# A two-layer decoder trunk: decay tables in another layout, the skip diagonal on ScalarE, and other hands for the last norms

## The chip, the cores and the metric

The kernel runs on one core of a Trainium2 chip. The metric is the device time of one execution in microseconds; before the change the median of three runs is 2406.37 us. Within a core five engines run their own instruction rows and meet at semaphores: TensorE (PE, matrix products), VectorE (DVE), ScalarE (ACT), GpSimd (POOL) and SyncE (SP, which issues DMAs).

## The reference, cut to what matters

The input x is 1024 tokens by 1024 channels, float32. The first layer is a diagonal state-space layer (S5), the second is stick-breaking attention; behind each stand a norm, a squared-ReLU MLP (1024 to 4096 to 1024) and another norm.

```python
def layer_norm(x, g, b):
    mu = jnp.mean(xf, axis=-1, keepdims=True)
    var = jnp.mean(jnp.square(xf - mu), axis=-1, keepdims=True)
    return (xf - mu) * lax.rsqrt(var + LN_EPS) * g + b

def s5_mixer(x, ...):
    u = (x @ w_in).reshape(bsz, seq, S5_GROUPS, S5_GROUP)      # 64 groups of 16 channels
    ...                                                        # a = exp(lambda dt), B scaled
    _, _, s_re, s_im = lax.associative_scan(combine, (a_re, a_im, bu_re, bu_im), axis=0)
    y = einsum(s_re, c_re) - einsum(s_im, c_im) + d_skip * u
    g = jax.nn.gelu(y)
    return (g * jax.nn.sigmoid(g @ w_glu + b_glu)) @ w_out

for layer in range(2):
    mix = s5_mixer(...) if layer == 0 else stick_breaking_attention(...)
    x = layer_norm(alpha * x + mix, ln_mix_g, ln_mix_b)
    ff = square(relu(x @ w1 + b1)) @ w2 + b2
    x = layer_norm(alpha * x + ff, ln_mlp_g, ln_mlp_b)
```

## The kernel before

Every float32 product is made of three matmuls on operands split into a high and a low part; `split` (L122 the cast of the high part on ScalarE, L123 the subtraction for the low part on VectorE) is the most used helper. The stages follow each other: the projection u (to 58.6 us of the profiled span), the S5 loop (to about 262), the gate (GLU, to 365), the projection `so` with its norms (to 457), the MLP of layer 0 (`m0` up, `d0` down, to about 1040 and its norms), K, V and attention (to 1650), the projection `ao` with its norms (to 1740), and the MLP of layer 1 (`m1` up, `d1` down). A scheduler orders each engine's row from the order of the code and the readiness of the operands; an engine then runs its row strictly in order.

**S5 loop.** The 64 groups are worked through in 16 halves of four groups (`Half`), two for each of eight indices i. Rotation tables C and S for index i come from `outer_tables(i)` (L480 to L491): four products and two sums of [128, 4, 8, 16] on VectorE, whose factors TA (8 powers) and TB (16 powers) are broadcast along the other's axis. TA and TB are built once (L413 to L420) by doubling, with `cmul` (L364 to L369: four products, a difference and a sum on VectorE) on 1, 2, 4 (and for TB 8) powers at a time for all NQ = 32 columns. They stand as [P, power, NQ], so that neighbouring powers lie 128 bytes apart.

A half's chain is: VT and WW (L526 to L528, VectorE, from the input coefficients), their transposes pv (TensorE) and copies V, Vs (L542 to L544, ScalarE), p = V x U (L590, L592, TensorE), R (L596 to L598, VectorE), the scan (L603, VectorE), Rs and Rc (L610, L611, VectorE), y (L616 to L619, TensorE), its gelu and its transposed output. Beside it, `decay` and `kern` make the short kernel matrix: a diagonal `di` [32, 4, 32] of d_skip values (L555, VectorE) and products of VT and WW are summed in the PSUM tile pk (L563 to L568) and copied into Dm (L576, four ScalarE copies), which the y products read. While the first six indices of the loop run, TensorE is filled up with matmuls of the projection u.

**Up-projection.** `mlp_up` multiplies with Strassen-like sums: `xo.first`, `xo.second` and `xo.third` transpose blocks of y into operands B.. and T.. of the products, `early(q)` is one 12-matmul product (M1 into bank A for even q, M2 into a bank of `psX` for odd q) made ahead of the main loop, while the norms of the last tiles still run. `xo.third` uses `psX` banks too.

**Down-projection and last norms.** `run` in the down stage makes products M1, M5, M6, M3, M7, M2, M4, each added by VectorE (`evict`, L1105) to the half tiles of y0..y7. Each norm has `stats` (L182, one per half tile), `center` (L187 to L190 on VectorE, the power on GpSimd, L192, the mean's subtraction on ScalarE, L194) and `scale` (L203 times rs and g, L204 plus b, both VectorE, then the DMA out, L206). In layer 1, y0..y3 are complete after M3 and their norms run under M7 and M4, from `queue`; y4..y7 follow as M4 ends bank by bank.

## Time and profile before

| | |
|---|---|
| median of 3 runs | 2406.37 us (2405.84 to 2408.62) |
| the profiled execution | 2409.81 us |
| its span, first to last instruction | 2408.1 us |
| mean granted TensorE clock | 0.981 |
| TensorE busy | 2283.8 us, 95% |
| VectorE busy | 1853.5 us, 77% |
| ScalarE busy | 1220.4 us, 51% |
| GpSimd busy | 409.1 us, 17% |

Rows are read so: a timeline row has start, duration, engine, line, operation, the tile written, the tiles read, the shape and, in brackets, how long the engine had waited for whom. Instructions of one engine overlap a little in the records, so that a step's true price is the distance to the next start.

### The profile page before, as it was taken

The numbers are of one execution on the slowest core, as the hardware profiler recorded it, in microseconds if no ns is written. First come the engines' busy times: TensorE is split into PE (matmuls) and PEld (weight loads), VectorE is DVE, ScalarE is ACT, GpSimd is POOL, SyncE is SP. The second block draws the span as 40 slices with busy tenths as digits, with TensorE's granted clock in tenths as the row PEclk, the third lists the DMA queues.
The fourth block names the chain that finished last, engine by engine and source line by source line (L and its number), as shares of the span: only waits on it lengthen the run. The fifth ranks groups of instructions, "written<-read, shape, count | busy, mean of one in ns | idle before, by whom it ended". The sixth has DMA issues, their size and how long they took to land.

```text
span 2408.1 us, 32696 instructions
## 1 busy us (share of the span) xinstructions
PE 2283.8 (95%) x11072; PEld 1873.7 (78%) x11072; DVE 1853.5 (77%) x2899; ACT 1220.4 (51%) x2299; POOL 409.1 (17%) x704
## 2 busy tenths in 40 slices
PE   9987899999999999999999999888989999999996
PEld 7777787777888788888887888766777888788885
DVE  7899674886665787789169999896887666687888
ACT  5455441465555444445156777663356555444443
POOL 4000140012111000001144434341002111100001
PEclk9998999999999999999999999999999999999998
DMA  4221232376444845437655554555457343665432
GB/s 147 61 78 47 60 111 66 136 257 206 145 144 149 303 134 154 148 97 192 123 134 117 129 122 109 119 140 192 139 173 280 147 152 145 228 201 167 135 110 105
DMA packets 195160, 349.38 MB, mean 145 GB/s; under 512 B 23216, under 2 KB 66224, under 8 KB 194992
## 3 DMA queue, kind: packets, MB, share of 16 engines
q1 hardware_dynamic: 136112, 246.61, 32.4%
q0 software_dynamic: 58880, 100.69, 15.1%
q8 instruction: 87, 1.43, 0.3%
q14 instruction: 81, 0.66, 0.1%
HBM read 212.96 MB, written 100.66 MB: 130 GB/s over the span
## 4 chain that ended last, share of the span: by engine, by line
PE 65%; DVE 16%; issue 9%; DMA 4%; ACT 3%; POOL 2%; SPq 0%; POOLq 0%; DVEq 0%; ACTq 0%
PE d0M L1096 4%; PE d0M L1097 4%; PE d0M L1098 4%; PE d1M L1096 4%; PE d1M L1098 4%; PE d1M L1097 4%; DVE qq L1447 2%; PE m0A L832 2%; PE m0A L833 2%; PE m0A L834 2%; PE m1A L832 2%; PE m1A L834 2%; PE m1A L833 2%; DVE be L1448 2%; PE po L1474 2%
## 5 line engine op out<-in xcount | busy, mean ns | idle before, releaser
L1447 DVE TENSOR_TENSOR_SCAN qq<-qq 128x128 f32<-128x128 f32 (+7 forms) x128 | 173.7, 1359 | 12.1 <-POOL qq L1441 11.9
L1096 PE MATMUL d1M<-w_d12M,w_d1HM 128*128 128x512 f32 x448 | 175.7, 393 | 3.9 <-DVE d1y L1105 3.9
L1098 PE MATMUL d1M<-w_d12M,w_d1HM 128*128 128x512 f32 x448 | 175.9, 393 | 0.0
L1096 PE MATMUL d0M<-w_d02M,w_d0HM 128*128 128x512 f32 x448 | 174.7, 391 | 1.2 <-DVE d0y L1105 1.2
L1097 PE MATMUL d1M<-w_d12M,w_d1HM 128*128 128x512 f32 x448 | 175.4, 392 | 0.0
L1097 PE MATMUL d0M<-w_d02M,w_d0HM 128*128 128x512 f32 x448 | 174.8, 390 | 0.0
L1098 PE MATMUL d0M<-w_d02M,w_d0HM 128*128 128x512 f32 x448 | 174.6, 390 | 0.0
L122 ACT CAST w_d1HM<-d1hM 128x512 fp32r<-128x512 f32 x110 | 68.3, 621 | 170.1 <-PE d1M L1098 148.1
L122 ACT CAST w_d0HM<-d0hM 128x512 fp32r<-128x512 f32 x110 | 68.3, 621 | 169.0 <-PE d0M L1098 142.8
L122 ACT CAST wTh<-pt 128x512 fp32r<-128x512 f32 (+1 forms) x192 | 88.1, 486 | 84.1 <-PE pt L1460 83.6
L1460 PE MATMUL pt<-ident,be 128*128 128x128 f32 x576 | 91.2, 283 | 36.4 <-DVE wTl L123 28.0
L192 POOL TENSOR_TENSOR rsd<-ved,nhalf 128x1 f32<-128x1 f32 x16 | 16.2, 1014 | 621.1 <-DVE ved L190 612.9
L1460 PEld LDWEIGHTS pt<-ident,be 128*128 128x128 f32 x576 | 70.3, 144 | 62.1 <-issue 17.8
L123 DVE TENSOR_TENSOR w_d1HM<-d1hM,w_d1HM 128x512 fp32r<-128x512 f32 x110 | 75.8, 689 | 52.3 <-ACT w_d1HM L122 52.2
L123 DVE TENSOR_TENSOR w_d0HM<-d0hM,w_d0HM 128x512 fp32r<-128x512 f32 x110 | 75.9, 690 | 51.5 <-ACT w_d0HM L122 51.4
L123 DVE TENSOR_TENSOR wTl<-pt,wTh 128x512 fp32r<-128x512 f32 (+1 forms) x192 | 99.7, 545 | 11.5 <-ACT wTh L122 11.4
L1448 DVE TENSOR_TENSOR be<-be,qq 128x127 f32<-128x127 f32 (+7 forms) x128 | 99.4, 777 | 7.2 <-POOL be L1441 0.5
L1096 PEld LDWEIGHTS d1M<-w_d12M,w_d1HM 128*128 128x128 f32 x448 | 84.4, 188 | 24.1 <-ACT w_d12M L122 4.3
L1438 ACT ACTIVATE qq<-pz 128x512 f32<-128x512 f32 (+1 forms) x192 | 97.2, 507 | 10.9 <-DVE be L1448 5.3
L1096 PEld LDWEIGHTS d0M<-w_d02M,w_d0HM 128*128 128x128 f32 x448 | 84.1, 188 | 21.2 <-DVE d0y L1105 2.5
L1098 PEld LDWEIGHTS d1M<-w_d12M,w_d1HM 128*128 128x128 f32 x448 | 84.6, 189 | 18.4
L1097 PEld LDWEIGHTS d1M<-w_d12M,w_d1HM 128*128 128x128 f32 x448 | 84.6, 189 | 17.9
(480 smaller groups left out, 7084.5 us busy)
## 6 DMA issues: line engine op xcount, KB each, us to landing
d0hM<-h_d SPq DMA_DIRECT2D x110, 256.0 KB, 2.7
d1hM<-h_d SPq DMA_DIRECT2D x110, 256.0 KB, 2.7
x1ring<-in_w SPq DMA_DIRECT2D x70, 256.0 KB, 3.1
x3ring<-in_w SPq DMA_DIRECT2D x70, 256.0 KB, 3.2
h_d<-m0hs POOLq DMA_DIRECT2D x64, 256.0 KB, 2.8
h_d<-m1hs POOLq DMA_DIRECT2D x64, 256.0 KB, 2.8
d0r<-in_w SPq DMA_DIRECT2D x58, 256.0 KB, 3.7
d1r<-in_w SPq DMA_DIRECT2D x58, 256.0 KB, 3.3
```

The costliest lines, as they stand in the source:

```text
L122: act.copy(hi, src)
L123: dve.tensor_sub(lo, src, hi)
L832: pe.matmul(ps_, wh, xh[:, k], start=first and k == 0, stop=False, skip_group_check=True)
L833: pe.matmul(ps_, wh, xl[:, k], start=False, stop=False, skip_group_check=True)
L834: pe.matmul(ps_, wl, xh[:, k], start=False, stop=k == 3, skip_group_check=True)
L1096: pe.matmul(ps_, hh[:, tok(t)], wh, start=first, stop=False, skip_group_check=True)
L1097: pe.matmul(ps_, hh[:, tok(t)], wl, start=False, stop=False, skip_group_check=True)
L1098: pe.matmul(ps_, hl[:, tok(t)], wh, start=False, stop=last, skip_group_check=True)
L1438: act.activation(qq[:, s0:s1], pz, AF.Sigmoid, scale=-0.125)
L1447: dve.tensor_tensor_scan(out=rev, data0=rev, data1=rev, initial=1.0, op0=ALU.mult, op1=ALU.bypass)
L1448: dve.tensor_mul(be[:, 0:ns - 1], be[:, 0:ns - 1], qq[:, 1:ns])
L1460: pe.transpose(pt[:, b_], self.be[:, tok(s0 + b_)], ident)
```

## The change

1. TA and TB become [P, NQ, power]: the inner index of `outer_tables` is adjacent; `cmul` writes and reads them through a rearranged view.
2. `di` is written by four ScalarE activations of [32, 32] (the identity times a per-partition d_skip) instead of one VectorE product of [32, 128].
3. In `mlp_up`, `early(1)` stands before `xo.third(..., 4)` and `early(2)` before `xo.third(..., 5)`.
4. Last norms of both down stages: the statistics of the halves n = 0 of y0..y3 run when M5's products are issued (`bnst` gets 8 buffers), only the other half's after the last sum.
5. Last norms of layer 1 only: g is copied by ScalarE into two PSUM tiles, the scaling runs in halves with g from there; the bias of y0..y4 is added by GpSimd (one 128x1024 instruction), that of y5..y7 by VectorE in halves with a DMA for each. g and b are loaded at M2 rather than M3, and the entries of `queue` are spread over eight units.

```diff
 class LayerNorm:
-        def __init__(self, pl, y, g, b, nm, last=False, dst=None):
+        def __init__(self, pl, y, g, b, nm, last=False, dst=None, gp=None, late=False):
...
-            self.st = pl.tile([P, 2, 6], F32, tag="bnst", name=f"st{nm}", bufs=4)
+            self.gp, self.late = gp, late
+            self.st = pl.tile([P, 2, 6], F32, tag="bnst", name=f"st{nm}", bufs=8)
...
         def scale(self):
             y = self.y
-            for c in self.parts():
+            for h in range(2) if self.gp else ():
+                c = half(h)
+                dve.scalar_tensor_tensor(y[:, c], y[:, c], self.rs, self.gp[h], op0=ALU.mult, op1=ALU.mult)
+                if self.late:
+                    dve.tensor_add(y[:, c], y[:, c], self.b[:, c])
+                    dma.dma_start(self.dst[:, c], y[:, c])
+            if self.gp and not self.late:
+                pool.tensor_add(y, y, self.b)
+                dma.dma_start(self.dst, y)
+            for c in self.parts() if not self.gp else ():
                 dve.scalar_tensor_tensor(y[:, c], y[:, c], self.rs, self.g[:, c], op0=ALU.mult, op1=ALU.mult)
                 dve.tensor_add(y[:, c], y[:, c], self.b[:, c])
...
-        TA = [sp.tile([P, 8, NQ], F32, name=f"TA{x}") for x in range(2)]
-        TB = [sp.tile([P, 16, NQ], F32, name=f"TB{x}") for x in range(2)]
+        TA = [sp.tile([P, NQ, 8], F32, name=f"TA{x}") for x in range(2)]
+        TB = [sp.tile([P, NQ, 16], F32, name=f"TB{x}") for x in range(2)]
         for tab, n_, s0 in ((TB, 4, 1), (TA, 3, 5)):
+            tab = [v.rearrange("p q a -> p a q") for v in tab]
...
-            a_ = [v[:, :, qs].rearrange("p a q -> p q a").unsqueeze(3).to_broadcast(sh) for v in TA]
-            b_ = [v[:, :, qs].rearrange("p b q -> p q b").unsqueeze(2).to_broadcast(sh) for v in TB]
+            a_ = [v[:, qs].unsqueeze(3).to_broadcast(sh) for v in TA]
+            b_ = [v[:, qs].unsqueeze(2).to_broadcast(sh) for v in TB]
...
-                dve.tensor_mul(di[self.hh][0:32], ident[0:32, 0:32].unsqueeze(1).to_broadcast([32, 4, 32]),
-                               dsk[:, self.g0:self.g0 + 4].unsqueeze(2).to_broadcast([32, 4, 32]))
+                for q in range(4):
+                    act.activation(di[self.hh][0:32, q], ident[0:32, 0:32], AF.Copy,
+                                   scale=dsk[:, self.g0 + q:self.g0 + q + 1])
...
         early(0)
+        early(1)
         xo.third(psX, "p", y_tiles, 4)
         rest[0]()
         w_early(4, wb)
         w_early(5, wb)
-        early(1)
         rest[1]()
+        early(2)
         xo.third(psX, "p", y_tiles, 5)
-        early(2)
...
             def ln(t):
-                lns[t] = LayerNorm(cp, self.y[t], gb[0], gb[1], f"{nm}{t}", t == 7, (out if self.last else x2_d)[tok(t)])
+                lns[t] = LayerNorm(cp, self.y[t], gb[0], gb[1], f"{nm}{t}", t == 7,
+                                   (out if self.last else x2_d)[tok(t)], gp, t > 4)
             def ln_a(t):
-                if t not in lns:
-                    ln(t)
-                    lns[t].stats()
+                lns[t].stats(1)
                 lns[t].center()
...
-                if fin and m == "M3" and q == 0:
+                if fin and m == "M2" and q == 0:
                     gb = [bcast(cp, A[f"lnf{x}"][l], f"{nm}{x}") for x in "gb"]
...
-                        queue = [[(ln_a, 0)], [(ln_a, 1), (ls, 0)], [(ln_a, 2), (ls, 1)], [(ln_a, 3), (ls, 2)],
+                        gp = [psC.tile([P, HF], F32, tag="p", name=f"{nm}g{h}") for h in range(2)]
+                        for h in range(2):
+                            act.copy(gp[h], gb[0][:, half(h)])
+                        for t in range(4):
+                            lns[t].gp = gp
+                        queue = [[(ln_a, 0)], [(ls, 0)], [(ln_a, 1)], [(ls, 1)], [(ln_a, 2)], [(ls, 2)], [(ln_a, 3)],
                                  [(ls, 3)]]
...
                         lns[4 + t].center()
+                        for f, a in queue.pop(0) if queue else ():
+                            f(a)
...
-                    for t in range(2 if then else 4, 8):
+                    for t in range(4, 8):
...
+                if fin and m == "M5":
+                    ln(q)
+                    lns[q].stats(0)
```

ScalarE's row in the S5 loop, around the twelfth half (V and Vs: its transposed coefficients; W_11 copies of WW; Dm_117: its kernel matrix; gs: gelu), before:

```order
219 L543 COPY Vs_2069<-pv_2063 128x4x64
220 L544 ACTIVATE Vs_2069<-pv_2063 128x4x64
221 L626 ACTIVATE gs_2033<-gs_2033 128x512
222 L573 COPY W_11_2168<-WW_2073 64x512
223 L574 ACTIVATE W_11_2168<-WW_2073 64x512
224 L622 ACTIVATE gs_2156<-py_2143 128x512
225 L642 ACTIVATE gT_h_1638<-pz_2203 128x512
226 L576 COPY Dm_117<-pk_2158 32x512
```

and now:

```order
244 L568 ACTIVATE di_113<-ident,dsk 32x32
245 L554 COPY V_2101<-pv_2096 128x512
246 L555 COPY Vs_2102<-pv_2096 128x4x64
247 L556 ACTIVATE Vs_2102<-pv_2096 128x4x64
248 L639 ACTIVATE gs_2066<-gs_2066 128x512
249 L568 ACTIVATE di_113<-ident,dsk 32x32 x3
250 L586 COPY W_11_2204<-WW_2106 64x512
251 L587 ACTIVATE W_11_2204<-WW_2106 64x512
252 L568 ACTIVATE di_114<-ident,dsk 32x32
253 L589 COPY Dm_117<-pk_2194 32x512
```

The diagonals of two halves stand between the other copies, single ones directly ahead of V and of Dm.

TensorE's row at the start of m1 (m1A and m1B: the first two products, ptx3T: the transposes of `xo.third`), before, from the end of the first product on:

```order
7076 L834 MATMUL m1A_16504<-x3B_15830,w_m_00_16369 128x512
7077 L239 MATMUL ptx3T_16517<-ident,y_0_15822 128x128 x4
7078 L239 MATMUL ptx3T_16524<-ident,x3t_16409 128x128 x4
7079 L239 MATMUL ptx3T_16531<-ident,y_4_15826 128x128 x4
7080 L239 MATMUL ptx3T_16538<-ident,y_0_15822 128x128 x4
7081 L832 MATMUL m1A_16607<-x3B_15830,w_m_20_16403 128x512
...
7084 L832 MATMUL m1B_16558<-x3B_15831,w_m_10_16386 128x512
```

and now:

```order
7075 L847 MATMUL m1A_16552<-x3B_15878,w_m_00_16417 128x512
7076 L845 MATMUL m1B_16565<-x3B_15879,w_m_10_16434 128x512
...
7087 L847 MATMUL m1B_16565<-x3B_15879,w_m_10_16434 128x512
7088 L250 MATMUL ptx3T_16580<-ident,y_0_15870 128x128 x4
7089 L250 MATMUL ptx3T_16587<-ident,x3t_16457 128x128 x4
7090 L250 MATMUL ptx3T_16594<-ident,y_4_15874 128x128 x4
7091 L250 MATMUL ptx3T_16601<-ident,y_0_15870 128x128 x4
7092 L845 MATMUL m1A_16627<-x3B_15878,w_m_20_16451 128x512
```

The m1B product stands ahead of the four transposes instead of behind them.

VectorE's row at the end, between M7 and M4, before (d1y_19279 and d1y_19280: y0 and y1, 19283 and 19284: y4 and y5; w_d1HM and w_d12M: the low parts of operands of M4):

```order
2832 L203 SCALAR_TENSOR_TENSOR d1y_19279<-d1y_19279,rsd_21753,d1g 128x1024
...
2835 L204 TENSOR_TENSOR d1y_19279<-d1y_19279,d1b 128x1024
2836 L123 TENSOR_TENSOR w_d1HM_21793<-d1hM_21724,w_d1HM_21793 128x512
2837 L123 TENSOR_TENSOR w_d12M_21797<-d1r_21133,w_d12M_21797 128x512
...
2839 L203 SCALAR_TENSOR_TENSOR d1y_19280<-d1y_19280,rsd_21785,d1g 128x1024
...
2842 L204 TENSOR_TENSOR d1y_19280<-d1y_19280,d1b 128x1024
2843 L123 TENSOR_TENSOR w_d1HM_21826<-d1hM_21756,w_d1HM_21826 128x512
2844 L1105 TENSOR_TENSOR d1y_19283<-d1y_19283,d1M_21285 128x512
2845 L1105 TENSOR_TENSOR d1y_19284<-d1y_19284,d1M_21286 128x512
```

and now (y0 is d1y_19327, y4 and y5 are 19331 and 19332):

```order
2818 L206 SCALAR_TENSOR_TENSOR d1y_19327<-d1y_19327,rsd_21811,d1g_21789 128x512
2819 L206 SCALAR_TENSOR_TENSOR d1y_19327<-d1y_19327,rsd_21811,d1g_21790 128x512
2820 L123 TENSOR_TENSOR w_d1HM_21841<-d1hM_21780,w_d1HM_21841 128x512
2821 L123 TENSOR_TENSOR w_d12M_21845<-d1r_21181,w_d12M_21845 128x512
...
2824 L123 TENSOR_TENSOR w_d1HM_21869<-d1hM_21814,w_d1HM_21869 128x512
2825 L1118 TENSOR_TENSOR d1y_19331<-d1y_19331,d1M_21333 128x512
2826 L1118 TENSOR_TENSOR d1y_19332<-d1y_19332,d1M_21334 128x512
```

The scaling of y1 and both bias adds no longer stand ahead of the evictions of y4 and y5.

GpSimd's row at the end, before it is eight powers rsd one after the other, and now:

```order
696 L194 TENSOR_TENSOR rsd_21811<-ved_21808,nhalf 128x1
697 L211 TENSOR_TENSOR d1y_19327<-d1y_19327,d1b 128x1024
698 L194 TENSOR_TENSOR rsd_21866<-ved_21863,nhalf 128x1
699 L211 TENSOR_TENSOR d1y_19328<-d1y_19328,d1b 128x1024
700 L194 TENSOR_TENSOR rsd_21929<-ved_21926,nhalf 128x1
701 L211 TENSOR_TENSOR d1y_19329<-d1y_19329,d1b 128x1024
702 L194 TENSOR_TENSOR rsd_21948<-ved_21945,nhalf 128x1
703 L194 TENSOR_TENSOR rsd_21971<-ved_21968,nhalf 128x1
704 L194 TENSOR_TENSOR rsd_21980<-ved_21977,nhalf 128x1
705 L211 TENSOR_TENSOR d1y_19331<-d1y_19331,d1b 128x1024
706 L194 TENSOR_TENSOR rsd_22003<-ved_22000,nhalf 128x1
707 L211 TENSOR_TENSOR d1y_19330<-d1y_19330,d1b 128x1024
```

The five bias adds stand between the powers; the powers of y4 (rsd_21948) and of y7 (behind the last row) stand behind adds.

## Rows read from the trace of the kernel before

**Rows 1.** The page: busy time of the engines.

```profile
PE 2283.8 (95%) x11072; PEld 1873.7 (78%) x11072; DVE 1853.5 (77%) x2899; ACT 1220.4 (51%) x2299; POOL 409.1 (17%) x704
```

**Rows 2.** Windows of the S5 loop: length, busy PE PEld DVE ACT POOL, clock, DMA, GB/s.

```profile
58.60:100.00 41.40, 38.80 (x245) 32.25 (x246) 36.23 (x50) 16.51 (x33) 0.42 (x4) 0.96 0.25 61
100.00:165.00 65.00, 60.21 (x444) 51.17 (x441) 63.66 (x95) 38.25 (x78) 1.06 (x10) 0.97 0.27 72
165.00:262.00 97.00, 72.07 (x517) 66.29 (x518) 94.36 (x146) 52.15 (x109) 1.45 (x14) 0.83 0.21 52
```

**Rows 3.** Waits of TensorE from 58.6 to 262 us: total, times, longest.

```profile
PE py L617 <- DVE Rc L611: 11.0, 7, 4.0
PE py L616 <- ACT Dm L576: 10.1, 8, 1.7
...
PE p L590 <- ACT V L542: 2.4, 1, 2.4
```

**Rows 4.** Groups by shape: a table product, VT's product (ns minimum, median, maximum).

```profile
L490 DVE TENSOR_TENSOR ox<-TA,TB x8: 1041/1067/1107, 62.8 to 239.8; 128x512 f32<-128x512 f32 x8
...
L526 DVE TENSOR_TENSOR VT<-X,pb x16: 669/682/687, 42.5 to 253.3; 128x512 f32<-128x512 f32 x16
```

**Rows 5.** Groups by shape in the gate: a strided and an adjacent split.

```profile
L123 DVE TENSOR_TENSOR gg_l<-gt,gg_h x14: 1222/1425/2372, 298.1 to 356.9; 128x512 fp32r<-128x512 f32 x14
L123 DVE TENSOR_TENSOR w_glu<-r_glu,w_glu x12: 672/684/706, 293.2 to 319.5; 128x512 fp32r<-128x512 f32 x12
```

**Rows 6.** Groups by shape: the diagonal, copies of Dm, MLP activations with and without bias.

```profile
L555 DVE TENSOR_TENSOR di<-ident,dsk x16: 271/273/274, 33.2 to 254.6; 32x128 f32<-32x128 f32 x16
...
L576 ACT COPY Dm<-pk x64: 252/415/579, 78.2 to 269.6; 32x512 f32<-32x512 f32 x16, 32x384 f32<-32x384 f32 x16, 32x256 f32<-32x256 f32 x16, 32x128 f32<-32x128 f32 x16
...
L918 ACT ACTIVATE m1hA<-m1hA,b x48: 707/726/732, 1780.9 to 2073.5; 128x512 f32<-128x512 f32 x48
...
L919 ACT ACTIVATE m1hA<-m1hA x64: 614/632/647, 1782.0 to 2076.7; 128x512 f32<-128x512 f32 x64
```

**Rows 7.** TensorE at the starts of m0 (waits) and m1 (timeline).

```profile
PE m0B L832 <- DVE veso L189: 1.4, 1, 1.4
PE ptx1T L239 <- DVE x1B L123: 1.2, 1, 1.2
...
1753.13 0.80 PE L832 MATMUL m1B<-x3B,w_m 128*128 128x512 f32 x1 [5.78 <-DVE x3T L123]
1753.72 0.63 PE L833 MATMUL m1B<-x3B,w_m 128*128 128x512 f32 x1
```

**Rows 8.** Timeline of TensorE: ahead of M4, in M4, and its last matmul.

```profile
2375.90 0.47 PE L1096 MATMUL d1M<-w_d12M,w_d1HM 128*128 128x512 f32 x1 [2.92 <-DVE d1y L1105]
...
2377.19 0.63 PE L1097 MATMUL d1M<-w_d12M,w_d1HM 128*128 128x512 f32 x1
...
2388.41 0.39 PE L1098 MATMUL d1M<-w_d12M,w_d1HM 128*128 128x512 f32 x1
```

**Rows 9.** Timeline of VectorE and of GpSimd at the end.

```profile
2387.45 0.69 DVE L1105 TENSOR_TENSOR d1y<-d1y,d1M 128x512 f32<-128x512 f32 x1 [1.42 <-PE d1M L1098]
2388.06 1.22 DVE L204 TENSOR_TENSOR d1y<-d1y,d1b 128x1024 f32<-128x1024 f32 x1
2389.19 0.69 DVE L182 BATCH_NORM_STATS2 std<-d1y 128x6 f32<-128x512 f32 x1
...
2403.10 1.28 DVE L204 TENSOR_TENSOR d1y<-d1y,d1b 128x512 f32<-128x512 f32 x2
...
2391.34 0.55 POOL L192 TENSOR_TENSOR rsd<-ved,nhalf 128x1 f32<-128x1 f32 x1 [9.08 <-DVE ved L190]
2394.04 1.46 POOL L192 TENSOR_TENSOR rsd<-ved,nhalf 128x1 f32<-128x1 f32 x1 [2.15 <-DVE ved L190]
```

**Rows 10.** GpSimd's add in the gate (group by shape), and a VectorE product beside it.

```profile
L1310 POOL TENSOR_TENSOR zg<-gT_h,gT_l x16: 1289/1689/4660, 282.6 to 354.1; 128x512 f32<-128x512 f32 x16
...
303.22 1.77 DVE L1313 TENSOR_TENSOR gt<-gt,zg 128x512 f32<-128x512 f32 x1 [1.20 <-POOL zg L1310]
```

More of the change, by code (lines that the diff above doesn't have):

```diff
@@ L1127, in run @@
             lns, queue, tail = {}, [], []
-            gb = []
+            gb, gp = [], None
             def ln(t):
-                lns[t] = LayerNorm(cp, self.y[t], gb[0], gb[1], f"{nm}{t}", t == 7, (out if self.last else x2_d)[tok(t)])
+                lns[t] = LayerNorm(cp, self.y[t], gb[0], gb[1], f"{nm}{t}", t == 7,
+                                   (out if self.last else x2_d)[tok(t)], gp, t > 4)
             def ln_a(t):
-                if t not in lns:
-                    ln(t)
-                    lns[t].stats()
+                lns[t].stats(1)
                 lns[t].center()
@@ L1276, in run @@
             for t in (2, 3):
-                lns[t].stats()
+                lns[t].stats(1)
                 lns[t].center()
```

## The prediction

> **What bounds the kernel now.** I read the page's busy times first: TensorE is busy 95% of the span of 2408.1 us [rows 1]. So only the places where TensorE waits can pay, 2408.1 - 2283.8 = 124 us in all, 19.3 of them after the last matmul, which ends at 2388.8 [rows 8]. Next, the windows over the state-space loop (58.6 to 262 us), to see which engine fills it. VectorE works 36.2 of 41.4 us, then 63.7 of 65, then 94.4 of 97, while TensorE works 38.8, 60.2 and 72.1 at a granted clock of 0.96, 0.97 and 0.83 [rows 2]. From 100 us on VectorE is the bound, and TensorE idles 2.6 + 4.8 + 24.9 = 32.3 us. The waits list for that window tells who is late: the output products wait 11.0 us for Rc, the last VectorE step of a half, and 10.1 us for Dm, a ScalarE copy [rows 3]. ScalarE itself is busy 16.5 + 38.3 + 52.2 = 107 of 203 us [rows 2], but stands in the chain as a link. Last, the timelines of the two up-projections' starts and of the end [rows 7 to 9].
>
> **Tables.** Four of the six VectorE instructions of each outer_tables read TA or TB with the inner index 128 bytes apart. They take 1067 ns (one of the four lines stands in the rows, the others read alike, 8 instructions each, 32 in all); VT's product, of the same shape with adjacent data, takes 682 [rows 4]. With the inner index adjacent I take 1067 - 682 = 0.385 us off each: 32 x 0.385 = **12.3 us**, 1.54 for each of the eight tables. The price is the building of the tables: TB has 32+64+128+256 and TA 32+64+128 elements per partition and pass, six passes each, 4224 elements whose inner step becomes 32 or 64 bytes. No row shows that. The table products show 0.385 us over 512 elements = 0.75 ns an element for a strided input; a VectorE output with a stride, the split into gg_l, takes 1222 where the same operation on adjacent data takes 684 [rows 5], 1.05 ns an element. So the build costs 0 (short instructions may hide it) to 4.4 us; I take 4224 x 0.77 = **3.3 us**, since one strided operand is the nearer case. It lies at 46 to 58 us, right ahead of the first half, whose first product waits 2.4 us for V already [rows 3].
>
> [...]
>
> **Skip diagonal.** One VectorE instruction of 273 ns goes from each half [rows 6]; the next instruction starts about 0.2 us after it, so 16 x 0.2 = **3.2 us** leave VectorE. Four ScalarE activations of 32x32 come. The nearest row is the Dm copies: the smallest, 32x128, takes 252 ns and the largest, 32x512, 579 [rows 6], 0.85 ns an element; a 32x32 would be 252 - 96 x 0.85 = 170 ns. In the MLP an activation with a per-partition operand takes 726 ns and one without 632 [rows 6], 94 ns more. So 0.17 to 0.30 us, 0.25 taken, x 64 = 16 us (11 to 19) on ScalarE. ScalarE has 96 us free in the loop, so I cost them at nothing. What is queued behind them: V and Dm of the next half; the order shows single ones ahead of V and ahead of Dm. Without the cover each costs its 0.25 us.
>
> **The loop's sum.** VectorE loses 12.3 + 3.2 - 3.3 = 12.2 us. Before 165 us TensorE has only 7.4 us of idle time to give, and fills it with projection matmuls that don't vanish; five tables, eight diagonals and the build lie there, 7.7 + 1.6 - 3.3 = 6.0, and I credit 4. After 165 us three tables (4.6) and eight diagonals (1.6) leave a VectorE that is 97% busy; but the chain waits on ScalarE as well, so I credit 4.5 of 6.2. Together **-8.5 us**, bounds -13 (all, with a cheap build) to -3 (chain-bound).
>
> **Starts of the up-projections.** In m1 TensorE waits 5.78 us before the first m1B product, for a transposed block whose split stands behind norms on VectorE, and then runs at half clock (a matmul is 0.63 us long in the records [rows 7], not 0.39 as at the end [rows 8]). Afterwards twelve m1B products, ready long before, run ahead of the transposes. The wait for the norms of tiles 6 and 7 doesn't vanish: only 12 x 0.23 = 2.8 us of work is moved into it. **-2.7 us**, bounds 0 to -6 (the clock never falls). In m0 the waits are 1.2 and 1.4 us [rows 7]: **-2 us**, bounds -3 to +4, since the reordering also moves weight loads and splits that later products wait for. In d0, TensorE shows no wait that the norms cause: 0, give or take 1.
>
> **The end.** From 2360 us on VectorE goes from one instruction to the next to its last, but for 1.42 us ahead of 2387.45 [rows 9]; TensorE waits 2.92 us at 2375.90 for an eviction that stands behind scale and bias of y0 and y1, and then loses 1.7 us more at half clock, eight matmuls 0.2 us longer each [rows 8]. Five bias adds leave VectorE; an add holds it 2389.19 - 2388.06 = 1.13 us [rows 9], so 5.65 us, and 2.4 us of statistics move under M5. But most of this lies before the last matmul. Of what VectorE does after it, only the adds of y3 and y4 go, 2.3 us. I laid out the new rows with the old spacings (0.6 for a half, 1.13 for an add, 0.06 for the small ones). The eviction comes some 3 to 4 us earlier, the last matmul at about 2384.5 (for 2388.8), and the last add, which ended at 2404.4 before [rows 9], ends at 2401.0 if GpSimd's adds disturb nothing and at 2402.3 if one of them holds up a split ahead of M4. GpSimd's price is not in the tail of before: its 128x512 add takes 1289 ns at least and 1689 at the median [rows 10], so 128x1024 is 2.6 to 3.4 us, and there the rs of y4 and y7 stand behind an add. I take **-2.1 us**, bounds -5 to +2. The two copies of g into PSUM (0.58 us each on ScalarE by the copy of 512 columns [rows 6]) lie ahead of casts with 0.3 us of slack, 0.
>
> What the rows show against it: while a GpSimd add of two SBUF tiles runs, VectorE's product of two SBUF tiles takes 1.77 us where such products take 0.68, and GpSimd's add up to 4660 ns for its 1289 [rows 4, 10]; and in the tail rs takes 1.46 us beside a bias add but 0.55 beside statistics [rows 9]. [...]
>
> **Sum.** -8.5 - 2 - 2.7 - 0 - 2.1 = -15.3 us. The profiled run took 2409.81 us (span 2408.1), so 2394.5 of its kind; the median of the timed runs is 3.4 lower at 2406.37, and I hold the difference: **2391 us**.
>
> **Rivals.** (1) *The loop gives little*: VectorE gets shorter, but the halves are bound by the chain V, p, R, scan, Rc, py and ScalarE's links in it, and the build is paid in full. Loop -2 to -3; total -8.8 to -9.8, **2396.6 to 2397.6**. For it: Dm waits are as large as Rc waits [rows 3]. Against it: VectorE is 97% busy, and a chain-bound loop would leave it gaps. (2) *Slower*: the 64 diagonal instructions land in ScalarE's row ahead of V and Dm, so that they are links of the chain. Price 16 us (up to 19) in the loop, the VectorE saving no longer counts, the rest of the change gives -6.8: 2406.4 + 16 - 6.8 = **2415.6**. It decides once more than 6.8 + 4.8 = 11.6 of the 16 us show, that is 0.7 us in every half. Against it: ScalarE idles 96 us in the loop, and most of the diagonals stand where it waits for py or pv. [...] (4) *The change doesn't do what it says*: tables read at the old price, as two broadcast operands may be slow by themselves. The diagonal still goes and the build still pays, loop -2 + 3.3; total 1.3 - 6.8 = -5.5, or -3.5 where m0 gives nothing: about **2402**. The row of VT, also a broadcast product [rows 4], speaks against it.
>
> **How the numbers follow.** Forecast 0.55 (2385 to 2395), better than that 0.10 (loop -13, m1 -6, end -5: down to 2380), rival 1 0.14, rival 3 0.08, rival 4 0.08, rival 2 0.05. A change of 0.2% (4.8 us) is about what a measurement can tell; below 2401.6 is faster. Rivals 1 and 3 are faster, 4 is the same, and 0.02 of rival 1 falls there too: faster 0.87 - 0.02 = 0.85, same 0.10, slower 0.05. The range leaves out rival 2, most of rival 4 and the far end: **2381 to 2401**. Its low end lies short of the sum of all the better bounds (-28), which won't come together; its high end is rival 1 with m0 at its +4.
>
> **What would show it.** Tables right: the four table products at 0.68 us; build right: TB and TA rows from 252 to about 300 to 450 ns. Loop: the last scan about 8 us earlier, TensorE's idle time between 165 and 262 us down from 25 to about 20. Diagonal wrong: py waiting for Dm more than 10.1 us. m1: the wait before the block's split at 3 us. End: wait of M4 under 1 us, VectorE's last add 16 to 19 us after the last matmul, rs of 0.55 us. The prediction is wrong if the loop ends less than 3 us earlier, or if a split ahead of M4 takes over 1.5 us.

## The result and the profile after

Over six runs beside six of the kernel before, the changed kernel takes 2389.01 us (2384.99 to 2393.1) against 2406.70 (2401.05 to 2408.62): ratio 0.9937, 95% interval 0.9924 to 0.9951, or 17.7 us less at the medians. A second set of runs (after_again below) gave 0.9931 (0.9917 to 0.9944). The profiled execution has a span of 2391.4 us, 16.8 less than before.

Where the 16.8 us lie, from the first and last matmul of each stage in the two timelines:

| stretch | before, us | after, us | difference |
|---|---|---|---|
| start to the first product of `so` (head, S5 loop, gate) | 362.9 | 353.8 | -9.1 |
| `so` and m0, to the first product of d0 | 426.7 | 424.7 | -2.0 |
| d0 and V, to the first transpose of attention | 436.1 | 437.0 | +0.9 |
| attention and `ao` | 514.1 | 511.4 | -2.8 |
| m1, to the first product of d1 | 335.6 | 333.2 | -2.5 |
| d1 and the end of the span | 332.7 | 331.4 | -1.4 |

The windows of the S5 loop, of after, answer to [rows 2] (length, busy PE, PEld, DVE, ACT, POOL, granted clock, DMA share, GB/s):

```profile
58.60:100.00 41.40, 40.70 (x262) 33.49 (x263) 35.66 (x54) 20.00 (x45) 0.43 (x4) 0.96 0.26 62
100.00:165.00 65.00, 61.03 (x457) 51.54 (x455) 61.50 (x95) 44.12 (x106) 1.17 (x11) 1.00 0.31 80
165.00:262.00 97.00, 74.94 (x556) 68.74 (x555) 89.42 (x138) 59.26 (x139) 1.58 (x15) 0.84 0.21 52
```

VectorE is down from 94.4 to 89.4 of 97 us in the last stretch, part of which is already the gate: between the first and the last scan it is busy 171.5 of 183.0 us, before 184.0 of 192.0, so that it is still the busiest engine there. ScalarE carries 14 to 21% more. TensorE idles 22.1 us between 165 and 262 us, 24.9 before; I had asked for about 20. The waits of TensorE from 58.6 to 262 us, of after, beside [rows 3]:

```profile
PE py L630 <- DVE Rc L624: 15.9, 5, 4.6
PE py L629 <- ACT Dm L589: 5.7, 7, 1.7
PE pv L552 <- ACT Dm L589: 4.1, 5, 1.7
```

TensorE waits longer than before for Rc (15.9 for 11.0 us). For Dm it waits less at py (5.7 for 10.1) and a little more at pv (4.1 for 3.2), together 9.8 for 13.3. Why the wait for Rc grew no run shows; the loop is shorter all the same.

The groups by shape, of after: a product of the tables, a step of their building with the same step of before, and the diagonal ([rows 4], [rows 6]).

```profile
L498 DVE TENSOR_TENSOR ox<-TA,TB x8: 678/682/692, 59.5 to 227.5; 128x512 f32<-128x512 f32 x8
...
L377 DVE TENSOR_TENSOR TB<-cm,cm x4: 204/322/615, 44.1 to 50.4; 128x32 f32<-128x32 f32 x1, 128x64 f32<-128x64 f32 x1, 128x128 f32<-128x128 f32 x1, 128x256 f32<-128x256 f32 x1
...
L568 ACT ACTIVATE di<-ident,dsk x64: 304/305/322, 24.9 to 236.3; 32x32 f32<-32x32 f32 x64
```

```profile
L366 DVE TENSOR_TENSOR TB<-cm,cm x4: 188/254/427, 46.6 to 51.7; 128x32 f32<-128x32 f32 x1, 128x64 f32<-128x64 f32 x1, 128x128 f32<-128x128 f32 x1, 128x256 f32<-128x256 f32 x1
```

The product takes 682 ns for 1067, the time of VT's product, as forecast. The longest step of the building (256 elements) takes 615 for 427 ns, 0.73 ns an element; over 4224 elements 3.1 us.

The start of m1, of after (timeline of TensorE), beside [rows 7]:

```profile
1737.25 1.11 PE L250 MATMUL ptx3T<-ident,y 128*128 128x128 f32 x4 [3.36 <-ACT m1kM L871]
...
1747.17 0.50 PE L845 MATMUL m1B<-x3B,w_m 128*128 128x512 f32 x1 [1.84 <-DVE x3T L123]
```

The one wait of 5.78 us has become two, 3.36 and 1.84. The first is new: the transposes now follow m1B and want a bank that ScalarE must first copy out (m1kM, L871). So the waits for the block and the bank together fell by 0.6 us only. Another wait at the start of m1 went altogether, one of 1.9 us for the norms (waits of TensorE, of before):

```profile
PE ptx3T L239 <- DVE y L757: 1.9, 1, 1.9
```

With 0.3 us that stayed, the start of m1 waits 5.5 us in place of 8.0: 2.5 us less, as much as the row of m1 in the table shows.

The end, of after: timeline of VectorE, then of GpSimd, then the wait ahead of M4 ([rows 8], [rows 9]).

```profile
2354.87 2.90 DVE L123 TENSOR_TENSOR w_d12M<-d1r,w_d12M 128x512 fp32r<-128x512 f32 x1
...
2373.77 0.75 DVE L206 SCALAR_TENSOR_TENSOR d1y<-d1y,rsd,d1g 128x512 f32<-128x512 f32 x1 [1.53 <-POOL rsd L194]
...
2380.00 2.40 DVE L208 TENSOR_TENSOR d1y<-d1y,d1b 128x512 f32<-128x512 f32 x2
...
2387.07 0.69 DVE L208 TENSOR_TENSOR d1y<-d1y,d1b 128x512 f32<-128x512 f32 x1
```

```profile
2354.48 2.73 POOL L211 TENSOR_TENSOR d1y<-d1y,d1b 128x1024 f32<-128x1024 f32 x1 [2.19 <-ACT w_d12M L122]
...
2370.88 2.35 POOL L211 TENSOR_TENSOR d1y<-d1y,d1b 128x1024 f32<-128x1024 f32 x1 [2.99 <-DVE ved L192]
2373.18 0.55 POOL L194 TENSOR_TENSOR rsd<-ved,nhalf 128x1 f32<-128x1 f32 x1
```

```profile
2359.23 0.47 PE L1109 MATMUL d1M<-w_d12M,w_d1HM 128*128 128x512 f32 x1 [1.62 <-DVE d1y L1118]
```

Three places show GpSimd's adds in VectorE's way. The split at 2354.87 takes 2.90 us for its 0.68: the add that began 0.4 us before it ended at 2357.21, and the split 0.56 us after that, so that it ran about its own length once the add was done; the rs of y4 runs only after the add of y2, and VectorE waits 1.53 us for it; two adds at 2380.00 take 2.40 for 1.28 us. The wait ahead of M4 is down from 2.92 to 1.62 us. The last matmul ends at 2370.7 and the last add at 2387.8, 17.1 us behind it (15.6 before). (The down stage makes its products in the order M1, M2, M5, M6, M3, M7, M4, and not in the one given ahead of the prediction. So M2 comes before M3, and the halves n = 0 of y0 to y3 are whole when M5 is issued.)

### The profile page after: what moved, and what is told of

The parts are those of the page before. It is cut to its first block, busy times and chain, and to the rows that moved or that the text cites. A ratio compares the mean times of both kernels' runs of the same rounds, so it can differ in the third digit from the quotient of the medians.

```text
span 2391.4 us, 32754 instructions
## 1 busy us (share of the span) xinstructions
PE 2276.9 (95%) x11072; PEld 1864.7 (78%) x11072; DVE 1838.9 (77%) x2887; ACT 1234.1 (52%) x2365; POOL 415.7 (17%) x709
## 4 chain that ended last, share of the span: by engine, by line
PE 59%; DVE 14%; issue 12%; DMA 5%; ACT 4%; POOL 4%; SPq 0%; POOLq 0%; DVEq 0%; ACTq 0%
PE d0M L1109 4%; PE d0M L1111 4%; PE d0M L1110 4%; PE d1M L1109 4%; PE d1M L1111 4%; PE d1M L1110 4%; DVE qq L1470 2%; PE m0A L847 2%; PE m0A L846 2%; PE m0A L845 2%; DVE be L1471 2%; POOL h_d L939 2%; PE po L1497 1%; PE pg L108 1%; PE pg L110 1%
## 5 line engine op out<-in xcount | busy, mean ns | idle before, releaser
L1470 DVE TENSOR_TENSOR_SCAN qq<-qq 128x128 f32<-128x128 f32 (+7 forms) x128 | 173.8, 1360 | 11.4 <-POOL qq L1464 11.2
L123 DVE TENSOR_TENSOR w_d1HM<-d1hM,w_d1HM 128x512 fp32r<-128x512 f32 x110 | 75.8, 690 | 52.5 <-ACT w_d1HM L122 52.2
L194 POOL TENSOR_TENSOR rsd<-ved,nhalf 128x1 f32<-128x1 f32 x16 | 11.3, 710 | 602.8 <-DVE ved L192 593.6
L123 DVE TENSOR_TENSOR w_d0HM<-d0hM,w_d0HM 128x512 fp32r<-128x512 f32 x110 | 75.8, 689 | 51.6 <-ACT w_d0HM L122 51.5
L1110 PEld LDWEIGHTS d1M<-w_d12M,w_d1HM 128*128 128x128 f32 x448 | 84.1, 188 | 17.7
```

The lines of the kernel that those rows point to most:

```text
L123: dve.tensor_sub(lo, src, hi)
L1110: pe.matmul(ps_, hh[:, tok(t)], wl, start=False, stop=False, skip_group_check=True)
L1470: dve.tensor_tensor_scan(out=rev, data0=rev, data1=rev, initial=1.0, op0=ALU.mult, op1=ALU.bypass)
```

## The experiments

Each was timed in five or six runs (before_sq in eleven) beside the kernel before on the same chip; the ratio is to those runs. Diffs are against the changed kernel, except where said.

| kernel | median, us | ratio to before, 95% | first and last scan start, us | d1 and end, us |
|---|---|---|---|---|
| before | 2406.70 | | 75.5, 267.5 | 332.7 |
| changed | 2389.01 | 0.9937 (0.9924 to 0.9951) | 74.1, 257.1 | 331.4 |
| after_again | 2388.65 | 0.9931 (0.9917 to 0.9944) | 74.1, 253.4 | 331.2 |
| no_tables | 2394.29 | 0.9957 (0.9940 to 0.9974) | 72.3, 261.3 | 331.3 |
| no_di | 2388.52 | 0.9931 (0.9914 to 0.9948) | 70.4, 252.5 | 330.8 |
| no_mlp | 2394.74 | 0.9952 (0.9936 to 0.9968) | 74.3, 256.2 | 331.2 |
| no_norms | 2387.70 | 0.9929 (0.9911 to 0.9947) | 73.3, 252.8 | 331.2 |
| tabs_mlp | 2392.72 | 0.9944 (0.9930 to 0.9957) | 75.8, 256.2 | 333.0 |
| bias_dve | 2391.03 | 0.9939 (0.9926 to 0.9952) | 73.4, 254.3 | 332.8 |
| pool_halves | 2386.37 | 0.9918 (0.9904 to 0.9932) | 70.7, 251.5 | 329.3 |
| squares | 2392.88 | 0.9949 (0.9936 to 0.9962) | 76.3, 256.1 | 331.5 |
| before_sq | 2405.34 | 1.0003 (0.9993 to 1.0013) | 74.1, 263.6 | 332.8 |
| sq_pool | 2385.08 | 0.9915 (0.9903 to 0.9927) | 71.3, 250.7 | 331.4 |
| both_fixes | 2384.42 | 0.9914 (0.9901 to 0.9928) | 71.2, 250.5 | 329.5 |

**no_tables: the old layout.**

```diff
-        TA = [sp.tile([P, NQ, 8], F32, name=f"TA{x}") for x in range(2)]
+        TA = [sp.tile([P, 8, NQ], F32, name=f"TA{x}") for x in range(2)]
...
-            a_ = [v[:, qs].unsqueeze(3).to_broadcast(sh) for v in TA]
+            a_ = [v[:, :, qs].rearrange("p a q -> p q a").unsqueeze(3).to_broadcast(sh) for v in TA]
...
```

> The changed kernel with TA and TB in the old layout; all else as changed. In the changed kernel's trace the S5 loop and the gate end 9.07 us earlier (the projection so starts at 353.8 us, before at 362.9). Theory (VectorE bounds the loop and the tables carry most of it): the old layout gives back about two thirds, so starts at 359 to 361, total some 6 us above the changed kernel's 2389.0, 2394 to 2396. Rival 1 (the loop is bound by its chain, and the diagonal did it): so starts below 356.5, total within 2.5 us of 2389. Rival 2 (all of it is the tables, the diagonal on ScalarE costs what it saves): so starts at 362 or later, total 2397 to 2399. For the attention stage, which is 2.7 us shorter in the changed kernel's trace though the change doesn't touch it: if it is chance, its length here lies anywhere between 424.8 us (changed) and 427.6 us (before).

The scans, of no_tables:

```profile
L615 DVE TENSOR_TENSOR_SCAN R<-Mt,R x16: 1204/1218/1225, 72.3 to 261.3; 128x512 f32<-128x512 f32 x16
```

`so` starts at 358.0 us, 4.2 later than in the changed kernel's first trace and 8.1 later than in its second (349.9), so the place of that start alone doesn't decide, and the bounds that I had set on it were too fine. The scans do: from the first to the last they take 189.0 us here, and 179.3 to 183.0 (mean 180.4) in the nine traces with new tables and the diagonal on ScalarE. The total is 5 to 6 us over the changed kernel's, as the theory had it. The two ratios' intervals overlap (0.9940 to 0.9974 and 0.9924 to 0.9951), but the fastest run here (2392.28) is slower than the slowest of no_di and of no_norms (2392.21 and 2391.22), which were timed beside it. The first scan comes at 72.3, where the five traces whose head differs only in the tables have 73.3 to 74.3. Before and tabs_mlp, which have the diagonal on VectorE, differ by 0.3 (75.5 and 75.8). So the building costs 0.3 to 2 us of the 3.1 that VectorE spends on it.

**no_di: the diagonal back on VectorE.**

```diff
-                for q in range(4):
-                    act.activation(di[self.hh][0:32, q], ident[0:32, 0:32], AF.Copy,
-                                   scale=dsk[:, self.g0 + q:self.g0 + q + 1])
+                dve.tensor_mul(di[self.hh][0:32], ident[0:32, 0:32].unsqueeze(1).to_broadcast([32, 4, 32]),
+                               dsk[:, self.g0:self.g0 + 4].unsqueeze(2).to_broadcast([32, 4, 32]))
```

> The changed kernel with the skip diagonal back on VectorE. Theory: 16 x 0.2 = 3.2 us come back to VectorE, 2 to 3 of them to the loop: so starts at 355.8 to 356.8, total 2391 to 2392. Rival (64 activations, 0.305 us each by the trace of the changed kernel, so 19.5 us on ScalarE, cost as much as they save): so starts at 352.5 to 354.5, total 2388 to 2390, and TensorE's waits for Dm and for V fall below the 9.8 and 0.3 us they have in the changed kernel.

The total is level (2388.52), which is the rival's and not the theory's. The rival's sign isn't there, though: TensorE waits 10.3 us for Dm (8.7 at py, 1.6 at pv), not less than the changed kernel's 9.8. The scans take 182.1 us. And this trace has a head of its own: its first scan starts at 70.4 us, 3.7 sooner. The reason is a GpSimd instruction in the head, the power that makes mag8 (the decay of a whole chunk, from which Mt is filled). Timeline of GpSimd, of no_di and of the changed kernel:

```profile
16.67 5.67 POOL L339 TENSOR_TENSOR mag<-ec,ex 128x32 f32<-128x32 f32 x1
```

```profile
16.96 15.36 POOL L339 TENSOR_TENSOR mag<-ec,ex 128x32 f32<-128x32 f32 x1
```

The program is the same there, and so are VectorE's rows beside it, back to back. What hangs on it shows in SyncE's queue (timeline of SP, of the changed kernel):

```profile
27.09 0.43 SPq L75 DMA_DIRECT2D b<-in_b  x1
32.35 1.81 SPq L477 DMA_DIRECT2D M<-mag  x3
34.26 0.53 SPq L133 DMA_DIRECT2D r_win<-in_w_in  x1
```

SyncE stands for 5 us at the DMA into M, until mag8 is there, and the loads of w_in behind it wait as well; in no_di that DMA goes at 27.4. Of ten traces that have this power, the one of before included, eight show 15.4 to 16.6 us and two 5.7. The diagonal's place doesn't decide it: of the two short ones no_di has it on VectorE and pool_halves on ScalarE.

**no_mlp: the old order of early products.**

```diff
         early(0)
-        early(1)
         xo.third(psX, "p", y_tiles, 4)
...
         w_early(5, wb)
+        early(1)
         rest[1]()
-        early(2)
         xo.third(psX, "p", y_tiles, 5)
+        early(2)
```

> The changed kernel with the old order of the early products and transposes in both up-projections. Theory: m0 and the start of m1 owe their gains (1.8 to 2.0 and 2.5 us) to that order alone: from the last product of so to the last of m0 322.5 us become 324.4, from the last of ao to the last of m1 333.5 become 336, total 2393 to 2394. In m1 TensorE again waits over 5 us ahead of the first m1B product. Rival (the gain in m0 or m1 comes from weights that arrive at another time, not from the order): one of the two stages keeps its length within 0.5 us, total 2389 to 2391.

The total is 2394.74, 6 us over the changed kernel. The waits of TensorE in no_mlp, at the start of m1 and in m0:

```profile
PE m1B L845 <- DVE x3T L123: 5.8, 1, 5.8
PE ptx3T L250 <- DVE y L770: 1.8, 1, 1.8
...
PE m0A L845 <- ACT m0kM L926: 3.2, 1, 3.2
```

The 5.8 us are back. From the last product of `so` to d0 it takes 334.1 us; the old order in before and before_sq takes 332.7 twice, the new order 330.7 in the changed kernel's trace, 332.9 in no_di and 328.2 to 329.8 in the nine others. So m0's usual gain is about 4 us, and the trace that I first read had the smaller one. Part of it is the wait for m0kM in the middle of m0 (2.3 us in before, 3.2 here), which the new order doesn't show; a wait for VectorE's m0hA, 2.4 us in the changed kernel's trace and 0.7 in before, takes back some of it. m1 takes 333.8 us from `ao` to d1 here and 334.4 to 335.8 in before and before_sq, against 332.2 to 335.0 (mean 333.8) with the new order: about 1 us on the mean, which is less than one trace differs from the next, and 2.5 in the trace of the result. For m1 the theory therefore missed: to its last product it had 336 us here, and it is 334.0, within 0.5 of the changed kernel's 333.5, which was the rival's sign. The total's gain lies in m0. (The ratio's interval overlaps that of the changed kernel here too.)

**no_norms: the last norms as before** (`LayerNorm` and the down stage of the kernel before; the rest as changed).

```diff
-                        queue = [[(ln_a, 0)], [(ls, 0)], [(ln_a, 1)], [(ls, 1)], [(ln_a, 2)], [(ls, 2)], [(ln_a, 3)],
+                        queue = [[(ln_a, 0)], [(ln_a, 1), (ls, 0)], [(ln_a, 2), (ls, 1)], [(ln_a, 3), (ls, 2)],
                                  [(ls, 3)]]
...
-                if fin and m == "M5":
-                    ln(q)
-                    lns[q].stats(0)
```

> The changed kernel with the last norms of both down stages as before (no half statistics ahead, g from its SBUF tile, all biases on VectorE); tables, diagonal and order of the up-projections as changed. In the changed kernel's trace d1 and the end give 1.3 us and the stretch from d0's last product to attention loses 0.9. Theory: both come from the norms, so this kernel ends d1 some 1.3 us later and starts attention 0.9 us sooner: total within 1 us of 2389.0. Rival 1 (the end gains more than it seems, GpSimd's adds free VectorE by 5.6 us): total 2392 to 2393. [...]

The total is 2387.70, 0.3 below the theory's range, but d1 with the end takes 331.2 us, as long as with the new norms. Attention starts 436.3 us after d0's first product, against 437.0 and 436.7 in the changed kernel's traces and 436.1 in before: 0.4 to 0.7 of the 0.9 us. In before, before_sq and tabs_mlp the same old norms take 332.7 to 333.0. The difference is the clock: all four traces wait 2.9 us ahead of M4, but the granted clock of the last 15 us of products is 0.89 in before, before_sq and tabs_mlp and 1.00 here. Windows of before_sq and of no_norms:

```profile
2364.50:2379.50 15.00, 12.68 (x48) 9.98 (x48) 13.79 (x22) 2.83 (x4) 2.90 (x2) 0.89 0.17 70
```

```profile
2348.80:2363.80 15.00, 12.09 (x52) 9.28 (x50) 15.00 (x25) 3.33 (x4) 3.04 (x2) 1.00 0.22 90
```

From the end of that wait to the last matmul's end it is 12.7 to 12.9 us in those three and 11.3 here. With the shorter wait (1.6 us) the clock is 1.00 there in all eight traces that have it. So the new norms give about 1.5 us where the clock fell behind the wait and nothing where it did not, the latter by one trace: in this run the last matmul came later than with the new norms, and the end behind it was shorter by as much (19.4 for 20.7 us).

**tabs_mlp: the kernel before with tables and order alone** (against the kernel before).

```diff
-        TA = [sp.tile([P, 8, NQ], F32, name=f"TA{x}") for x in range(2)]
+        TA = [sp.tile([P, NQ, 8], F32, name=f"TA{x}") for x in range(2)]
...
         early(0)
+        early(1)
         xo.third(psX, "p", y_tiles, 4)
...
```

> The kernel before with only the table layout and the order of the early products changed; skip diagonal on VectorE, last norms as before. Theory: the diagonal and the norms give nothing once the tables are short, so this kernel is as fast as the whole change, 2387 to 2390. From the first scan to the last 179 to 182 us (192.0 before, 183.0 and 179.3 in the two traces of the changed kernel). Rival (diagonal and norms carry 3 to 5 us together): 2392 to 2394. If the short second power of GpSimd in no_di's head (5.7 us, not 15.4) belongs to the diagonal's place and not to chance, it is short here too and the first scan starts near 70.4.

At 2392.72 the total is where the rival had it, 3.7 to 4.1 us over the changed kernel's two medians (1.7 to 3.1 by the ratios, whose intervals overlap). Its scans take 180.4 us, the mean of the nine traces with the diagonal on ScalarE, so this trace shows no gain of the diagonal inside the loop once the tables are short; with the old tables no_tables stands 3.0 below before and 0.5 below before_sq. The power in the head is long here (16.5 us) and the first scan starts at 75.8, against 73.3 to 74.3 in the five traces of the changed loop with a long power: on ScalarE the diagonals give about 2 us in the head where the power is long. Where it is short they give nothing there: no_di, with the diagonals on VectorE, starts its first scan at 70.4, and pool_halves, with them on ScalarE, at 70.7. d1 and the end take 333.0 us. Against after_again the first scan starts 1.7 us later and the end is 1.9 longer, about the 3.4 us by which the spans differ (2390.3 and 2386.9).

**after_again: the changed kernel unaltered.**

> The changed kernel unaltered, beside the next three on the same chip. [...] Rival (the spread comes from TensorE's clock falling at other places): the times spread evenly, and first scan starts of equal height go with different totals.

The power was long here too (16.63 us) and the first scan started at 74.1, yet the span is 4.5 us shorter than in the first trace. 3.9 of them are there by the start of `so`, and they arise after the tenth scan, which starts at 184.1 in both. Windows of the changed kernel and of after_again:

```profile
175.00:200.00 25.00, 19.86 (x149) 18.41 (x148) 23.69 (x38) 14.30 (x33) 0.41 (x4) 0.84 0.22 54
200.00:225.00 25.00, 17.95 (x140) 16.32 (x139) 24.52 (x40) 16.24 (x40) 0.43 (x4) 0.85 0.22 53
```

```profile
175.00:200.00 25.00, 19.92 (x154) 18.42 (x154) 24.65 (x40) 15.29 (x35) 0.41 (x4) 0.88 0.23 54
200.00:225.00 25.00, 17.90 (x146) 16.10 (x146) 24.95 (x40) 16.73 (x43) 0.42 (x4) 0.93 0.22 53
```

My theory had been that the spread of one kernel's times comes from this power alone, 5.7 us long in some executions and 15.4 to 16.1 in others. It falls: equal first scans go with different totals, and the granted clock of the thinly filled stretch (0.84 and 0.85 against 0.88 and 0.93) goes with it, as the rival said. That the clock causes the difference, and is not itself lowered by what makes the loop longer, no run shows. The length of the power is a second source, not the source. VectorE fills 24.65 and 24.95 of the 25 us in after_again, so it still bounds this stretch.

**squares and before_sq: mag8 by three products on VectorE** (before_sq: the same on the kernel before).

```diff
-        pool.tensor_tensor(mag8, ec, ex8, op=ALU.pow)
+        dve.tensor_mul(mag8, mag, mag)
+        dve.tensor_mul(mag8, mag8, mag8)
+        dve.tensor_mul(mag8, mag8, mag8)
```

> The changed kernel with mag8 = mag to the 8th made by three VectorE products of 128x32 instead of the second GpSimd power. Theory: Mt is ready by 27 us in every execution, ScalarE's casts of w_in no longer wait for it, the first scan starts at 69 to 71 us (74.1 in the changed kernel's trace), total 2384 to 2386, and the spread of the five times shrinks to about 4 us. Rival (the late Mt hides behind the projection, or another step of the head is next late): first scan still at 73 to 74, total within 1.5 us of the unaltered kernel's.

> The kernel before with the same replacement of mag8. Theory: first scan at 71 to 72 us (75.5 in the trace of before), total 3 to 5 us under the kernel before, near the lower group of its runs (2402), spread about 4 us; the distance to the changed kernel with the replacement is what the change gives without this source of chance, 14 to 17 us. Rival as there: no gain.

Both missed. The first of the three products stands early in VectorE's row and waits there for mag (timeline of VectorE, of squares):

```profile
17.30 0.19 DVE L339 TENSOR_TENSOR mag<-mag 128x32 f32<-128x32 f32 x1 [4.67 <-POOL mag L338]
```

The stall of 5 us on SyncE was traded for one of 4.67 us on VectorE, and the whole head moved: first scan at 76.3, total 4 us slower than unaltered. This did not tell the theories apart; the next one does.

**sq_pool: the same three products on GpSimd.**

```diff
-        pool.tensor_tensor(mag8, ec, ex8, op=ALU.pow)
+        pool.tensor_tensor(mag8, mag, mag, op=ALU.mult)
+        pool.tensor_tensor(mag8, mag8, mag8, op=ALU.mult)
+        pool.tensor_tensor(mag8, mag8, mag8, op=ALU.mult)
```

> The changed kernel with mag8 as three GpSimd products of mag (128x32) in place of the second wide power; in squares the three stood on VectorE, where the first of them held the row up for 4.7 us until mag was there, so that run did not tell. Theory: mag8 is ready by 20 us in place of 32.3, SyncE's DMA into M, behind which the loads of w_in queue, goes at 27.4 as in no_di, the first scan starts at 70 to 71 us in place of 74.1, total 2384 to 2387. Rival (the start of the loop hangs on something else): first scan at 73 to 74, total 2388 to 2390.

Timeline of GpSimd, of sq_pool:

```profile
16.47 10.29 POOL L339 TENSOR_TENSOR mag<-mag 128x32 f32<-128x32 f32 x1
26.84 0.24 POOL L340 TENSOR_TENSOR mag<-mag 128x32 f32<-128x32 f32 x1
27.16 0.24 POOL L341 TENSOR_TENSOR mag<-mag 128x32 f32<-128x32 f32 x1
```

mag8 was not ready by 20 us, as I had written, but at 27.4, just in time for the DMA at 27.57; the first scan starts at 71.3, the total is 2385.08 (2382.8 to 2388.1), 3.6 us under after_again, though the two ratios' intervals still touch (0.9903 to 0.9927 and 0.9917 to 0.9944). The start of the loop does hang on this DMA. The first of three equal products takes 10.29 us and the two behind it 0.24: the instruction is not slow, it is kept waiting. VectorE's row shows until when. It runs without a gap to 26.66 us, stands for 0.59 us, and the product ends 0.10 us into that gap; in the changed kernel's first trace the gap starts at 27.03 and the power ends 5.3 us later, near the 5.67 us that it takes in no_di. Timelines of VectorE, of sq_pool and of the changed kernel:

```profile
27.25 0.19 DVE L391 TENSOR_TENSOR pwi<-mag,sn 128x32 f32<-128x32 f32 x1 [0.59 <-ACT sn L368]
```

```profile
27.73 0.19 DVE L389 TENSOR_TENSOR pwi<-mag,sn 128x32 f32<-128x32 f32 x1 [0.70 <-ACT sn L366]
```

All six traces with a long power and such a gap (0.07 to 1.39 us) show the same 5.3 us. Before and tabs_mlp, with the diagonal on VectorE, have no such gap, and the power ends at 33.8 and 33.2 us instead of 32.0 to 32.9.

**bias_dve and pool_halves: who adds the biases, and in what pieces.**

```diff
-                pool.tensor_add(y, y, self.b)
+                dve.tensor_add(y, y, self.b)
```

> The changed kernel with the biases of y0 to y4 added by VectorE (128x1024) instead of GpSimd; g still comes from PSUM in halves. In the changed kernel's trace the three places where GpSimd's adds hold VectorE up are a split at 2354.9 us (2.3 us too long, before M4), a wait of 1.5 us for rs behind an add at 2373.8, and two adds at 2380.0 (1.1 us too long). Theory (adds on GpSimd save 5.6 us of VectorE and lose about 4.9 in these three places): d1's first product to the span's end takes 331.4 us with GpSimd and 331 to 333 here. [...] Rival 2 (the saving is real, the waits fill idle time only): 335 or more.

```diff
-                pool.tensor_add(y, y, self.b)
-                dma.dma_start(self.dst, y)
+                for h in range(2):
+                    c = half(h)
+                    pool.tensor_add(y[:, c], y[:, c], self.b[:, c])
+                    dma.dma_start(self.dst[:, c], y[:, c])
```

> The changed kernel with GpSimd's five bias adds split into halves of 128x512, each with its own DMA. Theory (a GpSimd add keeps VectorE's two-input instructions and its own later powers waiting for its whole length, 2.35 us): holds of half the length, so the split ahead of M4 takes under 2 us in place of 2.9 for its pair, TensorE's wait ahead of M4 falls from 1.6 to about 0.6 us and d1's first product to the span's end from 331.2 to 329.5 to 330.5 us. Rival (VectorE's row, not the holds, sets the end): 331 or more.

The waits of TensorE ahead of M4, of bias_dve and of pool_halves:

```profile
PE d1M L1109 <- DVE d1y L1118: 0.5, 1, 0.5
```

```profile
PE d1M L1111 <- DVE d1y L1120: 1.2, 1, 1.2
```

With the biases on VectorE, M4 starts with hardly a wait, but from the last matmul to the span's end it is 23.3 us instead of 20.7, and d1 with the end takes 332.8 us: 1.6 more than after_again. With the adds in halves the same stretch takes 329.3, 1.8 less. So GpSimd's adds save more than they hold up, as the theory had it, and 1.8 us of the 4.9 that they hold up were had back. The split ahead of M4 takes 1.78 us, under 2 as forecast; the wait ahead of M4 is 1.2 us, not 0.6, and most of the gain comes behind the last matmul (19.2 us to the end for 20.7). The halves also have a DMA each, and no run parts the two. Nor does an add hold up every two-input instruction of VectorE: in the changed kernel the eviction L1118 at 2371.38 us takes 0.67 us while the add of 2370.88 runs (2.35 us long). pool_halves' total also owes something to its head, where the power was short (first scan at 70.7).

**both_fixes: sq_pool and pool_halves together.**

> The changed kernel with mag8 as three GpSimd products (sq_pool) and GpSimd's biases in halves (pool_halves). Theory: the two are at opposite ends of the program and add up: 2 to 4 us at the head, 1.9 us at the end, 2382 to 2385, and under both the changed kernel and the kernel before. Rival (pool_halves owed its time to a short power in its head, 5.7 us, not to the halves): as sq_pool, 2385 to 2386.

2384.42 us (2379.2 to 2386.6): the fastest median of all, ratio 0.9914 (0.9901 to 0.9928) to before, 4 to 5 us under the changed kernel. Against sq_pool alone the totals don't tell (0.7 us); the stretch of d1 and the end does, 329.5 for 331.4 us.

## Why the prediction was right

The forecast was 2391 us, 2381 to 2401, faster; the runs gave 2389.0, and the sum of -15.3 stands beside -17.7 at the medians. The mechanism of the largest term, the table products, was right and is measured. That the sum came out so near is in part luck: m0 gave about 2 us more than its term and m1 about 1.7 less, and the totals do not show what the diagonal and the norms give. Each of the two taken back by itself leaves the total level (no_di 2388.52, no_norms 2387.70), both together cost 3.7 to 4.1 us (tabs_mlp), and the intervals reach 3 to 4 us to each side. (One slip in the sums: the range's high end, called rival 1 with m0 at +4, is 2402.6 to 2403.6 by its own terms, not 2401.) The steps, one by one:

- *Tables, VectorE's work*: right. 682 ns for 1067, and the building 3.1 us where I took 3.3. The stride cost 0.75 ns an element as an input of the products and costs 0.73 in the building.
- *Loop, -8.5*: right in the sum (-9.1 in the trace), from another split. The tables alone take the scans from a mean of 190.8 us (before, before_sq) to 181.3 (no_di, tabs_mlp), 9.5 us of 12.3. The diagonal gives 0.8 more on the mean, less than one trace differs from the next. It takes 2.6 us of work from VectorE (171.1 to 171.5 us busy between the scans for 173.8 and 173.9), but VectorE then waits longer for TensorE's p (2.9 to 5.3 us for 1.9 and 2.5). VectorE remains the busiest engine, at 94 to 95%. Ahead of the first scan the diagonal gives about 2 us where GpSimd's power is long and nothing where it is short; the building costs 0.3 to 2 us there.
- *Diagonal on ScalarE at no cost*: right as far as the waits show. An activation takes 0.305 us, at my upper bound, 19.5 us if all are added; four in a row take 0.95 us (at 24.95 us), 0.24 each, near the 0.25 taken. TensorE's waits for Dm fell from 13.3 to 9.8 us, they didn't rise: the slower rival fell.
- *m0, -2*: right in the trace, too small for the usual run (about -4, outside my bound of -3). I had priced the waits at the start; the wait for m0kM in the middle, which the new order removes too, I had not priced.
- *m1, -2.7*: -2.5 in the trace, about -1 on the mean of all. The step that I missed is the bank: the transposes wait 3.36 us for ScalarE to copy m1B out, so that the work moved into the old wait opened a new one.
- *The end, -2.1*: -1.4. rs takes about 0.55 us in six of its eight powers and the last add comes 17.1 us after the last matmul, as forecast; the wait ahead of M4 is 1.6 us, not under 1, because the held split cost 2.2 us more (2.90 for 0.68). No run shows the 1.3 us that the sum takes for one held split; it was my estimate. I had written that a split of over 1.5 us would make the prediction wrong; it took 2.9, and the total didn't suffer, since I had taken the value with one held split. GpSimd's 128x1024 add takes 2.35 us at the median of five (2.34 to 2.73), below my 2.6 to 3.4 but for the longest.
- *The end made worse by GpSimd's adds* (rival 3 of the chances, 0.08): the holds are there, and the end gains all the same. The split at 2354.87 ends 0.56 us after the add, about its own length. The holds sum to about 5 us, but they are not all on the path: with the adds on VectorE the stretch is 1.6 us longer (bias_dve).
- *Not forecast*: 2.8 us in attention, which the change doesn't touch. Attention from its first transpose to its last output product takes 427.6 us in before and 422.2 to 425.7 in the twelve experiments and the changed kernel, old code and new alike (before_sq: 423.5). The profiled execution of before was at the slow end; so was the whole of it (2409.8 us for a median of 2406.7). This part of the trace's 16.8 us is chance.

What stays open: why the granted clock falls in one execution of a program and not in the next, and why GpSimd's power takes 5.7 us in two traces of ten and 15.4 to 16.6 in the other eight, of which six have it end 5.3 us after the start of a gap in VectorE's row; both were seen, neither was set. Open too is what the diagonal and the norms give to the total.

## What to carry to other kernels

Where an engine is busy 97% of a stretch, price an edit to it from two rows of the same shape, one strided and one adjacent, and check what a second cut gives: here 9.5 us of scans came from the tables alone and 0.8 on the mean from the diagonal, whose freed time came back as waits. Look at the DMA queue of the head: here one small DMA stood 5 us for a late value, and the loads of w_in behind it stood as well. Moving the adds to GpSimd paid here (331.2 us for 332.8 with them on VectorE), and it paid more in halves with a DMA each (329.3), where an add takes 1.27 us in place of 2.35.
